# SwiGLU's token-tile features turned by VectorE and transfers, and three small moves between engines

## The chip, the core and the metric

The kernel runs on one core of one Trainium2 chip. The metric is the time of one execution on the device in microseconds (us); the median of three runs is given with their range. A profile is taken of one further execution; its times are counted from the start of its span. Engine names in it: PE is TensorE (PEld its weight loads), DVE is VectorE, ACT is ScalarE, POOL is GpSimd, SP is SyncE, which here only issues transfers. A "q" behind a name is the engine's queue of instructions.

## What is computed

Two layers work on 256 tokens of 1024 features, all in float32. Each layer has a token mixer (a gMLP in layer 0, an mLSTM with four heads in layer 1), then a dense SwiGLU of width 2816, then a gated embedding; behind the mixer and behind the SwiGLU stands a layer norm over a scaled residual:

```python
for i in range(DEPTH):
    y = gmlp_mixer(x, ...) if i % 2 == 0 else mlstm_mixer(x, ...)
    x = layer_norm(ALPHA * x + y, ln1_g[i], ln1_b[i])
    x = layer_norm(ALPHA * x + swiglu(x, ffn_w_gate[i], ffn_w_up[i], ffn_w_down[i]), ln2_g[i], ln2_b[i])
    gate = sigmoid(x @ ple_w_gate[i] + ple_b_gate[i])
    x = x + gate * (p[i] @ ple_w_proj[i])

def swiglu(x, w_gate, w_up, w_down):
    return (silu(x @ w_gate) * (x @ w_up)) @ w_down
```

In the mLSTM each head forms a masked 256 x 256 matrix P of queries against keys (scaled by exponentials of the gates), multiplies it with the values, divides by a sum, normalises, adds a skip path, and is gated with silu(z) before the output projection.

## The kernel before

**Precision.** Every float32 product is made of three matmuls in the fast 32-bit format: each operand is split into a high and a low half, and high x high, low x high and high x low are added in PSUM. `split` (L153) does it: ScalarE copies the value into the high half, VectorE subtracts to get the low half (`sub` names another engine for the subtraction, `fast=True` lets VectorE do the copy too).

**Weights.** `weight_plan` lists all weight tiles in the order of use. `ahead` (L170 on) issues their loads from SP into four `raw` buffers (L176, 512 KB each; the first three in halves of 256 KB), up to eight tiles ahead, and splits them into six `w` buffers or eight `b8` buffers, up to four tiles ahead. A load waits until its `raw` buffer has been split.

**Who sets the order.** The program is traced in Python, and a planner then gives each engine a fixed queue: among instructions that it holds ready by its own estimate it takes the one that comes first in the program, and it inserts the waits. `issue_after` and `manual_schedule` fix the order in a few places.

**The start.** After a few warm-up matmuls the input x, transposed on the host, comes in four pieces of two blocks (L359 on). ScalarE issues the load of block 0 (L363). `second_x` (L364) is called by `ahead` right after the first half of the first weight, so SP's queue begins: weight 0 first half, x block 1, weight 0 second half, x piece 1, weight 1 in two halves. L376 to L384 split these by hand: ScalarE copies x, VectorE or ScalarE copies the weight's half, VectorE subtracts. The matmuls at L422 use them.

**SwiGLU.** `channel_mixer` (L517). The first 512 of the 2816 features are made with tokens on the partitions: `first(t)` (L542) runs 48 matmuls for each token tile t of 128 tokens (gate, then up; the last eight of each at L289), and gives `hn[t]` = silu(gate) * up, 128 tokens x 512 features (L552, L553). The down projection needs features on the partitions. `transpose_h(t)` (L559) therefore transposes the four 128 x 128 blocks of `hn[t]` on TensorE into PSUM and splits each (128 x 128) into `hs[0..3]`. `transpose_h(0)` stands before the loop over f, `transpose_h(1)` after `gate_up(4)`. The other features, f = 4 to 21, are made by `gate_up(f)` with features on the partitions: eight matmuls each at L260 for `pg` and `pu`, then eight each at L264, then sums, silu, product and split. `Down` (L291 on) adds blocks into four PSUM banks at L240 to L242 (high, low, high of the activations); L240 and L242 load the high half of `h` as weights, L241 the low half. Blocks 0 to 3 are all added at f = 5, later blocks two steps behind `gate_up`.

**The mLSTM.** Under `manual_schedule` for ScalarE, L917 multiplies P of head h (128 x 384, causal blocks only) with its exponentials, and L920 splits it with the subtraction on GpSimd (`plo`). `pv_block(h)` (L930) multiplies with the values (L937 to L939; L939 takes `plo`), takes statistics on VectorE (L957 on), and lets ScalarE write the normalised `hn` (L967), which frees the PSUM banks `num`. `h_block(h)` (L971) transposes `hn` on TensorE (L976), adds the skip path on VectorE (L980), multiplies with silu(z) on VectorE (L981) and splits. `h_block(0)` runs behind `pv_block(2)`. After the last head, `Down` adds the 16 blocks; the first three wait for each other and are added together.

Of the kernel before, what the change touches and what calls it, by code (L numbers as in the profile page):

```python
# [12 lines left out]
ALU = mybir.AluOpType  # L13

P = 128
# [28 lines left out]
TOK = [slice(0, P), slice(P, 2 * P)]  # L44
# [11 lines left out]
def down_blocks(f):  # L56

    return range(4) if f == 3 + LAG else [f - LAG] if f > 3 + LAG else []
# [6 lines left out]
def stationary(key):  # L65

    return key[0] in ("u", "xm") and len(key) == 2 or key[0] in ("g", "u", "z") and key[-1] >= 4


def paired(key):  # L70

    return key[0] in ("g", "u") and len(key) == 3 and key[-1] >= 4 or key[0] == "u" and len(key) == 2
# [61 lines left out]
def trunk(ctx, tc, a, out):  # L134
    nc = tc.nc
    pe, act, dve, pool, sp = nc.tensor, nc.scalar, nc.vector, nc.gpsimd, nc.sync
# [8 lines left out]
    def tl(tag, shape, dt=F32, name="t"):  # L145
        return sb.tile(shape, dt, tag=tag, name=name, bufs=BUFS[tag])

    def bank(which, shape, name="ps"):
        return (psA if which == "A" else psB).tile(shape, F32, tag=which, name=name)

    def split(hi, lo, src, fast=False, sub=dve):

        return dve.tensor_copy(hi, src) if fast else act.copy(hi, src), sub.tensor_tensor(lo, src, hi.bitcast(F32), ALU.subtract)  # L153
# [14 lines left out]
    at = {"load": 0, "cast": 0, "use": 0}  # L168

    def ahead(loads, casts):  # L170
        while at["load"] < min(len(plan), at["use"] + loads):
            ap = plan[at["load"]][1]
            n = ap.shape[-1]
            t = tl("raw", [P, n], name="raw")
            for c in HALF if at["load"] < 3 else [slice(0, n)]:
                at["dma"] = sp.dma_start(t[:, c], ap[:, c])  # L176
                if at["load"] == 0 and c.start == 0:
                    second_x()
            raws[at["load"]] = t
            at["load"] += 1  # L180
        while at["cast"] < min(len(plan), at["use"] + casts):
            i = at["cast"]
            key, raw = plan[i][0], raws.pop(i)
            n = raw.shape[-1]
            if key in WIDE:
                t = tl("b8", [P, 2, D], F32R, "w")
            else:


                first = ASIDE if stationary(key) and not paired(key) else 0  # L190
                step = D + ASIDE if paired(key) else D
                t = tl("w", [P, 2 * D + P], F32R, "w")[:, first:first + 2 * step]
                t = t.rearrange("p (i n) -> p i n", i=2)[:, :, :D]
            with issue_after(behind["cast"]):
                if key[0] == "bdv":

                    t = t.rearrange("p i n -> p (i n)")[:, :4 * 2 * GW].rearrange("p (j i n) -> p j i n", j=4, i=2)
                    split(t[:, :, 0, :P], t[:, :, 1, :P], raw.rearrange("p (j n) -> p j n", j=4))
                    f = 4 * key[1]
                    pool.tensor_copy(t[:, :, :, P:], wx[:, f:f + 4, :].rearrange("p j (i n) -> p j i n", i=2))  # L200
                for c in () if key[0] == "bdv" else HALF if i < 3 else [slice(0, n)]:
                    split(t[:, 0, c], t[:, 1, c], raw[:, c])
            wt[i] = t
            at["cast"] += 1
# [18 lines left out]
    ident = sb.tile([P, P], F32, name="ident")  # L223
# [97 lines left out]
    def transpose_x(t):  # L321
# [5 lines left out]
            end = split(xh[:, 4 * j:4 * j + 4, TOK[t]], xl[:, 4 * j:4 * j + 4, TOK[t]], tp)  # L327
        return end

    def ln_residual(t, ps, g, b):  # L330
        x = xn[t]
        st = tl("c", [P, 2, 6], name="st")
        for j in range(2):
            c = HALF[j]
            dve.scalar_tensor_tensor(x[:, c], x[:, c], ALPHA, ps[j], ALU.mult, ALU.add)
            dve.bn_stats(st[:, j, :], x[:, c])
        mv = tl("c", [P, 2], name="mv")
        dve.bn_aggr(mv, st)
        rs = tl("c", [P, 1], name="rs")
        rsqrt(rs, mv[:, 1:2])  # L340
        for j in range(2):
            c = HALF[j]
            dve.scalar_tensor_tensor(x[:, c], x[:, c], mv[:, 0:1], g[:, c], ALU.subtract, ALU.mult)
            end = dve.scalar_tensor_tensor(x[:, c], x[:, c], rs, b[:, c], ALU.mult, ALU.add)
        behind["cast"] = (end,)

    def load_row(ap, n=D):
        t = tl("row", [P, n], name="row")
        sp.dma_start(t, ap.partition_broadcast(P))
        return t  # L350
# [7 lines left out]
    xr = []  # L358
    for i in range(4):  # L359
        t = tl("m2", [P, 2, S], name="xr")  # L360
        if i == 0:

            act.dma_start(t[:, 0, :], a["xT"][i, :, 0, :])  # L363
            second_x = lambda: sp.dma_start(xr[0][:, 1, :], a["xT"][0, :, 1, :])  # L364
            xr.append(t)
        else:
            sp.dma_start(t, a["xT"][i])
            xr.append(t)
        ahead(1 + i, 0)
    make_identity(nc, ident)  # L370
    pool.memset(mhalf, -0.5)
    with tc.manual_schedule(engines={mybir.EngineType.Activation, mybir.EngineType.DVE}):

        for i in range(2):
            w, raw = tl("w", [P, 2 * D + P], F32R, "w")[:, :2 * D].rearrange("p (i n) -> p i n", i=2), raws.pop(i)
            for k, h in enumerate(HALF):  # L376
                c = 2 * i + k
# [9 lines left out]
    for i in range(2, 4):  # L387
        c = slice(2 * i, 2 * i + 2)
# [4 lines left out]
    for c in range(6):  # L393
# [20 lines left out]
        for kp in range(4):  # L414
            w = weight("v", c, kp)
            for kk in range(2):
                k = 2 * kp + kk
# [11 lines left out]
        for t in range(2):  # L429
            o = vs[c][:, t, :]  # L430
# [22 lines left out]
    hs = {}  # L453
# [63 lines left out]
    def channel_mixer(l, acc, last, hook=None):  # L517
# [38 lines left out]
        hn = [first(0, lambda: transpose_x(1)), first(1)]  # L556
        hs = {e: tl("h", [P, 2, S], F32R, "h") for e in range(4)}

        def transpose_h(t):  # L559
            tp = bank("B", [P, 4, P], "tp")  # L560
            for e in range(4):
                pe.transpose(tp[:, e, :], hn[t][:, e * P:(e + 1) * P], ident)
            for e in range(4):
                split(hs[e][:, 0, TOK[t]], hs[e][:, 1, TOK[t]], tp[:, e, :])

        def gate_up(f):
            s, y = tl("s", [P, S], name="s"), tl("s", [P, S], name="y")
# [17 lines left out]
            hs[f] = tl("h", [P, 2, S], F32R, "h")  # L585
            split(hs[f][:, 0, :], hs[f][:, 1, :], s)

        transpose_h(0)
        rows = []
        for f in range(4, NF + LAG):  # L590
            if f < NF:
                gate_up(f)
            if f == 4:
                transpose_h(1)
                acc = Down(NF)
            for e in down_blocks(f):
                acc.add(e, hs.pop(e), weight("d", l, e, casts=1 if f >= NF else None))
            if f in (8, 10, 12):

                with issue_after([at["dma"]]):  # L600
                    rows.append(load_row(a[("ln2_g", "ln2_b", "ple_b")[f // 2 - 4]][l]))
            if f == 14 and hook:
                hook()
            if f == NF - 1:
                ahead(LOAD_AHEAD, LAG + 1)
# [96 lines left out]
    def mlstm(embed1):  # L702
# [32 lines left out]
        sz = [tl("b8", [P, 8, S], name="sz") for _ in range(2)]  # L735
# [97 lines left out]
        for s in range(NI + 3):  # L833
            if s < NI:
                y = xm_block(s)
# [23 lines left out]
        with tc.manual_schedule(engines={mybir.EngineType.Activation}):  # L859
# [43 lines left out]
            for h in range(NH):  # L903
                if h == 1:
                    z_copy(*z)
                    z = z_mm(11)
                gb = gbs[h // 2][:, h % 2]
                gm = tl("s", [P, 2, P], name="gm")
                dve.tensor_tensor(gm, gb, cmask.unsqueeze(1).to_broadcast([P, 2, P]), ALU.add)
                e = tl("m2", [P, 384], name="e")  # L910
                act.activation(e[:, 0:P], gm[:, 0, :], AF.Exp, bias=cols[:, 0, h:h + 1], scale=-1.0)
                act.activation(e[:, P:S], gb[:, 1, :], AF.Exp, bias=cols[:, 0, h:h + 1], scale=-1.0)
                act.activation(e[:, S:384], gm[:, 1, :], AF.Exp, bias=cols[:, 1, h:h + 1], scale=-1.0)
                if h == 1:
                    act.activation(cols[:, 2:4, :], cols[:, 2:4, :], AF.Exp, scale=-1.0)
                p = sc[h]
                dve.scalar_tensor_tensor(p, p, DH ** -0.5, e, ALU.mult, ALU.mult)  # L917
                hi = tl("h", [P, 384], F32R, "phi")
                lo = tl("h", [P, 384], F32R, "plo")
                split(hi, lo, p, sub=pool)  # L920
                ph.append((hi, lo))
            z_copy(*z)
            act.activation(sz[1][:, 0:4, :], sz[1][:, 0:4, :], AF.Silu)
# [1 line left out]
        hn = []  # L925
# [43 lines left out]
        hs = {}  # L969

        def h_block(h):  # L971
            for j in range(2):
                tp = bank("B", [P, 2, S], "tp")
                for i in range(2):
                    for t in range(2):
                        pe.transpose(tp[:, i, TOK[t]], hn[h][:, t, (2 * j + i) * P:(2 * j + i + 1) * P], ident)  # L976
                for i in range(2):
                    f = 4 * h + 2 * j + i
                    y = tl("s", [P, S], name="y")
                    dve.scalar_tensor_tensor(y, tp[:, i, :], par[:, f, 6:7], a1[f // 8][:, f % 8, :], ALU.mult, ALU.add)  # L980
                    dve.tensor_tensor(y, y, sz[f // 8][:, f % 8, :], ALU.mult)  # L981
                    hs[f] = tl("h", [P, 2, S], F32R, "h")
                    split(hs[f][:, 0, :], hs[f][:, 1, :], y)

# [119 lines left out]
```

## Time and profile before

| | |
|---|---|
| median of three runs | 825.69 us (825.42 to 826.16) |
| the profiled execution's own time | 825.63 us |
| its span | 823.9 us |
| granted TensorE clock, mean | 1.00 |
| bytes moved | 155.52 MB, 189 GB/s over the span |

The page gives, for each engine, the time in which it was busy, its share of the span and the number of its instructions. Matmuls are pipelined, so the busy times of single ones overlap: the distance between two starts says what one costs. The chain of waits follows back from the last instruction, at each step to what released it or to the instruction before it on its engine; its rows give start, length and what it was. In the timeline a row gives start, length, engine, line, operation, the tile written and the tiles read, and in brackets how long the engine had been idle before and what released it. A row of `SPq` is the issue of a transfer by SP; the time until the data has landed stands in the list of transfers.

### The profile page before, as it was taken

What the parts mean: (1) busy time and instruction counts of PE and PEld (TensorE: products, weight loads), DVE (VectorE), ACT (ScalarE), POOL (GpSimd) and SP (SyncE); (2) the same over time, 40 slices, a digit from 0 to 9 for tenths busy, and PEclk for the clock granted to TensorE, in tenths of its full rate; (3) what the DMA queues carried; (4) which work ended last, traced back from release to release, by engine and by line L of the source; (5) the groups of instructions that cost most, each with busy time, mean ns of one, the idle gap of its engine ahead of it and who ended that gap; (6) DMA issues with size and microseconds to landing.
All of it is one profiled execution on the core that took longest, in us unless ns stands there. A gap on an engine that the chain in (4) does not pass through costs nothing.

```text
span 823.9 us, 12407 instructions
## 1 busy us (share of the span) xinstructions
PE 816.9 (99%) x4520; PEld 708.0 (86%) x4520; DVE 614.3 (75%) x982; ACT 470.9 (57%) x820; POOL 149.6 (18%) x209
## 2 busy tenths in 40 slices
PE   9999999999999999999999999999999999999997
PEld 6888888888888888888889999988888888888886
DVE  6757998678956567586878998889885656776674
ACT  6656666565535556475256788776444555665522
POOL 1020643342000000700001677330000000000000
PEclk9999999999999999999999999999999999999999
DMA  8895447567176678677144355454626667886501
GB/s 287 283 337 182 153 159 225 179 194 243 67 260 202 192 225 281 201 229 252 38 146 156 135 162 161 146 177 147 215 90 224 196 199 228 269 264 212 179 1 51
DMA packets 44997, 155.52 MB, mean 189 GB/s; under 512 B 5256, under 2 KB 6024, under 8 KB 44936
## 3 DMA queue, kind: packets, MB, share of 16 engines
q1 hardware_dynamic: 44792, 154.60, 57.6%
q8 instruction: 35, 0.57, 0.3%
q14 instruction: 26, 0.21, 0.1%
q10 hardware_dynamic: 144, 0.13, 0.0%
HBM read 153.67 MB, written 1.05 MB: 188 GB/s over the span
## 4 chain that ended last, share of the span: by engine, by line
PE 96%; DVE 1%; ACT 1%; DMA 1%; issue 0%; POOL 0%; SPq 0%; DVEq 0%; ACTq 0%
PE acc L240 9%; PE acc L241 9%; PE acc L242 9%; PE pu L260 8%; PE pg L260 8%; PE ups L260 5%; PE pg L264 4%; PE pu L264 4%; PE ups L264 3%; PE vps L242 2%; PE vps L240 2%; PE vps L241 2%; PE xmps L245 2%; PE xmps L247 2%; PE xmps L246 2%; PE gate L289 2%
## 5 line engine op out<-in xcount | busy, mean ns | idle before, releaser
L153 DVE TENSOR_TENSOR w<-raw,w 128x1024 fp32r<-128x1024 f32 (+1 forms) x275 | 333.2, 1219 | 74.7 <-ACT w L153 73.1
L153 ACT CAST w<-raw 128x1024 fp32r<-128x1024 f32 (+1 forms) x275 | 284.9, 1046 | 120.6 <-PE acc L242 25.7
L240 PE MATMUL acc<-w,h 128*128 128x512 f32 x336 | 133.0, 396 | 0.2 <-ACT hn L967 0.2
L241 PE MATMUL acc<-w,h 128*128 128x512 f32 x336 | 131.3, 391 | 0.0
L242 PE MATMUL acc<-w,h 128*128 128x512 f32 x336 | 131.0, 390 | 0.0
L242 PEld LDWEIGHTS acc<-w,h 128*128 128x128 f32 x336 | 63.1, 188 | 13.9
L240 PEld LDWEIGHTS acc<-w,h 128*128 128x128 f32 x336 | 63.1, 188 | 12.1 <-ACT hn L967 0.6
L241 PEld LDWEIGHTS acc<-w,h 128*128 128x128 f32 x336 | 63.1, 188 | 11.2 <-DVE h L153 0.2
L260 PE MATMUL pg<-xs,w 128*128 128x512 f32 x288 | 71.6, 391 | 0.0
L260 PE MATMUL pu<-xs,w 128*128 128x512 f32 x288 | 71.5, 390 | 0.0
L260 PEld LDWEIGHTS pg<-xs,w 128*128 128x128 f32 x288 | 53.8, 188 | 11.0
L260 PEld LDWEIGHTS pu<-xs,w 128*128 128x128 f32 x288 | 53.8, 188 | 11.0
L319 POOL TENSOR_TENSOR rs<-ve,mhalf 128x1 f32<-128x1 f32 x8 | 7.6, 956 | 295.9 <-DVE ve L318 291.3
L271 ACT COPY s<-pg 128x256 f32<-128x256 f32 x36 | 13.4, 372 | 69.7 <-PE pg L264 69.7
L260 PE MATMUL ups<-xs,w 128*128 128x512 f32 x192 | 47.9, 391 | 0.0
L272 DVE TENSOR_TENSOR s<-s,pg 128x256 f32<-128x256 f32 x36 | 15.1, 421 | 42.8 <-ACT s L271 42.7
L260 PEld LDWEIGHTS ups<-xs,w 128*128 128x128 f32 x192 | 35.7, 188 | 7.2
L264 PEld LDWEIGHTS pg<-xs,w 128*128 128x128 f32 x288 | 38.9, 188 | 3.1
L264 PE MATMUL pg<-xs,w 128*128 128x256 f32 x288 | 39.5, 280 | 0.0
L264 PE MATMUL pu<-xs,w 128*128 128x256 f32 x288 | 39.4, 279 | 0.0
L264 PEld LDWEIGHTS pu<-xs,w 128*128 128x128 f32 x288 | 36.5, 188 | 0.3
L245 PE MATMUL xmps<-xs,w 128*128 128x256 f32 x128 | 36.3, 284 | 0.0
(252 smaller groups left out, 1635.7 us busy)
## 6 DMA issues: line engine op xcount, KB each, us to landing
raw<-in_ffn_g SPq DMA_DIRECT2D x44, 512.0 KB, 4.4
raw<-in_ffn_u SPq DMA_DIRECT2D x44, 512.0 KB, 4.6
raw<-in_ffn_d SPq DMA_DIRECT2D x44, 512.0 KB, 4.3
raw<-in_gm_u SPq DMA_DIRECT2D x24, 512.0 KB, 3.5
raw<-in_gm_wo SPq DMA_DIRECT2D x24, 512.0 KB, 3.4
raw<-in_gm_v SPq DMA_DIRECT2D x21, 512.0 KB, 5.2
raw<-in_ple_gate SPq DMA_DIRECT2D x16, 512.0 KB, 4.5
raw<-in_ml_z SPq DMA_DIRECT2D x16, 512.0 KB, 3.8
```

The costliest lines, as they stand in the source:

```text
L153: return dve.tensor_copy(hi, src) if fast else act.copy(hi, src), sub.tensor_tensor(lo, src, hi.bitcast(F32), ALU.subtract)
L240: pe.matmul(ps, lh, w[:, 0, c], start=start, stop=False)
L241: pe.matmul(ps, ll, w[:, 0, c], start=False, stop=False)
L242: pe.matmul(ps, lh, w[:, 1, c], start=False, stop=stop)
L245: pe.matmul(ps, w[:, 0, c], h, start=start, stop=False)
L246: pe.matmul(ps, w[:, 0, c], l, start=False, stop=False)
L247: pe.matmul(ps, w[:, 1, c], h, start=False, stop=stop)
L260: pe.matmul(ps, w[:, 0, k * P:(k + 1) * P], xs[:, k], start=k == 0, stop=False)
L264: pe.matmul(ps[:, 0], w[:, 1, k * P:(k + 1) * P], xh[:, k, :], start=False, stop=k == KD - 1)
L271: act.copy(o, ps[:, 1])
L272: dve.tensor_tensor(o, o, ps[:, 0], ALU.add)
L289: pe.matmul(ps, xl[:, k, TOK[t]], w[:, 0, c], start=False, stop=k == KD - 1)
```

## The change

Four edits:

1. **SwiGLU's token-tile features.** `transpose_h` goes, and its eight transposes on TensorE per layer with it. `square(y, t, hn[t])` is one VectorE instruction for each token tile: it transposes each 32 x 32 square of the 128 x 512 tile in place of its partition group, and orders the result by square column. `regroup` then moves the squares between partition groups with 16 transfers inside SBUF, issued by SP: each moves 32 partitions x 2 token tiles x 512 bytes, 32 KB. All 16 read what both squares wrote. The four splits (`split_h`, 128 x 256 each, from SBUF instead of PSUM) are placed after `gate_up(5)`, ahead of the blocks 0 to 3 of `Down`.
2. **P part of head 0.** The subtraction that gives the low half of P goes from GpSimd to VectorE for head 0.
3. **Gate of head 0.** The four multiplications with silu(z) go from VectorE to GpSimd for head 0.
4. **x's second block.** ScalarE issues its load, right behind that of the first; SP's queue loses it.

```diff
@@ ahead
             for c in HALF if at["load"] < 3 else [slice(0, n)]:
                 at["dma"] = sp.dma_start(t[:, c], ap[:, c])
-                if at["load"] == 0 and c.start == 0:
-                    second_x()
@@
+    def square(y, t, src):
+
+        dve.transpose(y[:, t].rearrange("p j k b -> p k j b"), src.rearrange("p (k j a) -> p k j a", k=4, j=4))
+
+    def regroup(o, y):
+
+
+        for j in range(4):
+            for i in range(4):
+                sp.dma_start(o[32 * j:32 * j + 32, :, i], y[32 * i:32 * i + 32, :, j])
@@ the start
         if i == 0:
-
-            act.dma_start(t[:, 0, :], a["xT"][i, :, 0, :])
-            second_x = lambda: sp.dma_start(xr[0][:, 1, :], a["xT"][0, :, 1, :])
+            for k in range(2):
+                act.dma_start(t[:, k, :], a["xT"][i, :, k, :])
@@ channel_mixer
-        def transpose_h(t):
-            tp = bank("B", [P, 4, P], "tp")
-            for e in range(4):
-                pe.transpose(tp[:, e, :], hn[t][:, e * P:(e + 1) * P], ident)
-            for e in range(4):
-                split(hs[e][:, 0, TOK[t]], hs[e][:, 1, TOK[t]], tp[:, e, :])
+
+        y = tl("row", [P, 2, 4, 4, 32], name="hsq")
+        for t in range(2):
+            square(y, t, hn[t])
+        ht = tl("row", [P, 2, 4, 4, 32], name="ht")
+        regroup(ht, y)
+
+        def split_h(e):
+            h = hs[e].rearrange("p i (t g b) -> p i t g b", t=2, g=4)
+            split(h[:, 0], h[:, 1], ht[:, :, :, e])
@@
-        transpose_h(0)
         rows = []
         for f in range(4, NF + LAG):
             if f < NF:
                 gate_up(f)
             if f == 4:
-                transpose_h(1)
                 acc = Down(NF)
+            if f == 5:
+                for e in range(4):
+                    split_h(e)
@@ mlstm
-                split(hi, lo, p, sub=pool)
+
+                split(hi, lo, p, sub=pool if h else dve)
@@ h_block
-                    dve.tensor_tensor(y, y, sz[f // 8][:, f % 8, :], ALU.mult)
+
+                    (dve if h else pool).tensor_tensor(y, y, sz[f // 8][:, f % 8, :], ALU.mult)
```

## The prediction

> **What bounds the kernel.** I read the page first (busy shares, chain by engine), then TensorE's waits, then the chain of waits, and the timeline around each edited place.
>
> ```profile
> span 823.9 us, 12407 instructions
> ...
> PE 816.9 (99%) x4520; PEld 708.0 (86%) x4520; DVE 614.3 (75%) x982; ACT 470.9 (57%) x820; POOL 149.6 (18%) x209
> ...
> PE 96%; DVE 1%; ACT 1%; DMA 1%; issue 0%; POOL 0%; SPq 0%; DVEq 0%; ACTq 0%
> ```
>
> TensorE works in 99% of the span and carries 96% of the chain. So only two things shorten the time: fewer TensorE instructions, and fewer of its waits. Those are few (engine, line <- releaser, total us, times, longest):
>
> ```profile
> PE vps L422 <- ACT w L382: 0.6, 1, 0.6
> PE num L939 <- POOL plo L153: 0.5, 1, 0.5
> ...
> PE acc L240 <- ACT hn L967: 0.2, 1, 0.2
> ```
>
> Each belongs to one of the small edits: the start, the P part of head 0, the gate. The big edit takes TensorE work away. The sum is made against the profiled execution, which took 825.63 us (span 823.9, and 1.73 around it); the median of the three runs shown, 825.69, is 0.06 from it. About 0.2%, 1.65 us, can be told from no change: below 824.04 is faster, above 827.34 slower.
>
> **Transposes taken from TensorE.** Each layer loses two groups of four transposes, ahead of `gate_up(4)` and ahead of the first `Down`. Busy time overstates them, since matmuls overlap; the chain shows what they hold up (start, us, what):
>
> ```profile
> 240.55 1.82 PE first L289 x8
> 242.81 1.85 PE pg L260 x8
> ...
> 247.43 0.94 PE pu L264 x8
> 248.80 1.84 PE pg L260 x8
> ...
> 265.24 1.81 PE pg L260 x8
> ...
> 630.84 1.82 PE first L289 x8
> 633.10 1.85 PE pg L260 x8
> ...
> 637.71 0.94 PE pu L264 x8
> 639.08 1.84 PE pg L260 x8
> ```
>
> From the end of one group to the start of the next: 242.81 - 242.37 = 0.44, 248.80 - 248.37 = 0.43, and in the second layer 0.44 and 0.43. The eight matmuls behind a transpose take 1.85 or 1.84 against 1.81 undisturbed (265.24), 0.03 or 0.04 each. Sum: 1.74 + 0.14 = **1.88 us less**, 0.94 in each layer. Nothing hides it: the engine goes straight on.
>
> **What replaces them.** Two passes of VectorE turn squares of 32, 16 transfers regroup the squares, and four splits (ScalarE copy, VectorE subtract) feed the first `Down` block at f = 5. All 16 need the second token tile's square, and block 0 needs all 16. Rows of the first layer:
>
> ```profile
> 242.48 0.69 DVE L553 TENSOR_TENSOR hn<-hn,first 128x512 f32<-128x512 f32 x1 [6.47 <-PE first L289]
> 243.08 1.22 DVE L153 TENSOR_TENSOR w<-raw,w 128x1024 fp32r<-128x1024 f32 x1
> ...
> 244.33 0.33 SPq L176 DMA_DIRECT2D raw<-in_ffn_g  x1
> ...
> 250.94 0.41 ACT L153 CAST h<-s 128x256 fp32r<-128x256 f32 x1
> ...
> 254.06 0.19 PEld L240 LDWEIGHTS acc<-w,h 128*128 128x128 f32 x1
> ...
> 254.18 0.19 PEld L241 LDWEIGHTS acc<-w,h 128*128 128x128 f32 x1
> ```
>
> Small loads issued back to back by SP, and times from issue to landing (last column) of a weight load, of the quickest load and of a store:
>
> ```profile
> 236.41 0.43 SPq L675 DMA_DIRECT2D wc<-in_ml_wc  x1
> 236.89 0.42 SPq L690 DMA_DIRECT2D wk<-in_ml_wk  x1
> ```
>
> ```profile
> raw<-in_ffn_g SPq DMA_DIRECT2D x44, 512.0 KB, 4.4
> ...
> raw<-in_ml_bdv SPq DMA_DIRECT2D x4, 256.0 KB, 2.7
> ...
> out<-xn SPq DMA_DIRECT2D x2, 128.0 KB, 1.7
> ```
>
> The last hn is ready at 242.48 + 0.69 = 243.17. No row shows a square; I give it the 0.69 of L553, the nearest pass over 128x512: 243.86. From 236.41 to 236.89 the queue needs 0.48 an issue, so the 16th goes out 15 x 0.48 = 7.2 later, near 251.1. No row shows a transfer within SBUF; 32 KB lies nearest to the 128 KB store, so 1.7: landed at 252.8. One copy (0.41, the cast at 250.94) and one subtract, taken the same: high half at 253.2, low half at 253.6. TensorE wants the low half (L241) at 254.18 - 0.94 = 253.24, so it waits **0.4 us**. The other blocks have 12 matmuls of cover each. In the second layer the two `pg` groups lie 5.98 apart as here (5.99), so the same 0.4; **0.8 in all**. Bounds: nothing, if the transfers land 0.4 sooner (less than nothing is excluded, the transposes are already booked); above, 1.22 for a square behind the queued weight subtract at 243.08, and 2.7 for landing like a weight load (4.4 - 1.7): 4.3 a layer.
>
> A rule of the Trainium skill speaks against this edit: "DMA: Bandwidth & Descriptors", section "Rules for kernel authors", wants small transfers joined into one, since under 64 KB mostly overhead is paid. Its "Anatomy of one DMA" puts the fixed part at about 2.0 us (for transfers issued by GpSimd), which would make the wait by my estimate 0.8 a layer, not 0.4, and the sum 0.8 us worse; no row here shows 32 KB within SBUF.
>
> Behind the 16 issues stand weight loads on SP. The one at 244.33 would go out near 251.6, land near 256.0 (4.4), and be cast and subtracted by about 258.4 (two passes at 1.22 at most); its matmuls start at 265.24 - 0.94 = 264.3. That cover of 5.9 makes the delay free. The splits themselves are no more work than the eight per layer that go.
>
> **P part of head 0.** Three timelines, VectorE with the gate's row below it, GpSimd, TensorE:
>
> ```profile
> 533.34 0.54 DVE L917 SCALAR_TENSOR_TENSOR sc<-sc,e 128x384 f32<-128x384 f32 x1
> ...
> 535.60 1.36 DVE L917 SCALAR_TENSOR_TENSOR sc<-sc,e 128x384 f32<-128x384 f32 x1
> ...
> 555.00 0.76 DVE L981 TENSOR_TENSOR y<-y,sz 128x256 f32<-128x256 f32 x2
> ```
>
> ```profile
> 534.50 2.04 POOL L153 TENSOR_TENSOR plo<-sc,phi 128x384 fp32r<-128x384 f32 x1 [11.40 <-ACT phi L153]
> ```
>
> ```profile
> 535.74 0.40 PE L938 MATMUL num<-vn,phi 128*128 128x512 f32 x1
> 536.60 0.50 PE L939 MATMUL num<-vn,plo 128*128 128x512 f32 x1 [0.47 <-POOL plo L153]
> 536.94 0.39 PE L937 MATMUL num<-vn,phi 128*128 128x512 f32 x1
> ```
>
> A matmul of this size takes a step of 0.23 (1.82 for eight, above), so L939 would start at 535.97 and L937 at 536.20; L937 starts at 536.94. So 0.74 is lost. On VectorE the subtract costs about 0.54 (L917, same size, alone): from 534.50 to 535.04, before 535.97. **0.74 less**; 0.4 if one weight pass of 1.22 stands ahead (535.72 + 0.54 = 536.26, a wait of 0.29, and its shadow); nothing gained is the end above.
>
> **Gate of head 0.** VectorE loses four multiplications, 0.76 for two, so 1.5 us, ahead of the last head's statistics, on which TensorE's wait of 0.2 for `hn` hangs. I take **0.2 less**; nothing is the end above. GpSimd's own price, by a pass of the same size, and the first `Down` matmul of this layer:
>
> ```profile
> L477 POOL TENSOR_TENSOR sv<-sv,cf 128x256 f32<-128x256 f32 x22 | 22.9, 1042 | 72.0 <-ACT sv L476 72.0
> ```
>
> ```profile
> 560.15 0.48 PE L240 MATMUL acc<-w,h 128*128 128x512 f32 x1
> ```
>
> Three such passes from 555.00 are over at 558.1, their splits (0.82) at 559.0, ahead of 560.15, and the fourth is used after these. But the L917 rows, 0.54 alone and 1.36 beside GpSimd's 2.04, show that the two slow each other. In the Trainium skill, "SBUF — State Buffer", section "Who interferes with whom", says that a VectorE operation with two SBUF inputs and a GpSimd operation reading SBUF exclude one another; by that rule, these rows agree. It is a rival below.
>
> **x's second block.** SP, the chain and VectorE at the start:
>
> ```profile
> 1.24 0.42 SPq L364 DMA_DIRECT2D xr<-in_xT  x1
> 1.71 0.42 SPq L176 DMA_DIRECT2D raw<-in_gm_v  x1
> ```
>
> ```profile
> 1.71 4.98 DMA raw<-in_gm_v
> ...
> 7.39 4.38 PE vps L422 x18
> ```
>
> ```profile
> 8.09 0.43 DVE L380 CAST w<-raw 128x512 fp32r<-128x512 f32 x1
> ```
>
> The half weight that ends the wait is issued 0.47 sooner. At most 0.47 comes of it. If the transfers behind land when they did, the 18 matmuls run into the next cast: six of 0.23 after 6.92 end at 8.30, the cast at 8.52, so 0.25 is kept. On the other side, a block of x that lands late puts its copy (0.41) ahead of the weight's. I take **0.2 less**.
>
> **Sum.** 825.63 - 1.88 - 0.74 - 0.2 - 0.2 + 0.8 = **823.4**.
>
> **Rivals.** (1) The regrouped squares come late, in part: landing at 2.7 like the quickest load, 1.0 later than taken, waits of 1.4 a layer, 2.8 in all: 825.4, no change. For it: the ring is shared with weight loads, and SP's pitch has no row for so scattered a pattern. Against: by 251 the queue has issued only these for 7 us.
> (2) Slower: the first `Down` block waits for transfers that stand behind weight loads. Square behind the subtract at 243.08 (1.22), landing 4.4: 4.3 a layer, 8.6 in all, 831.2. It decides once the low half is later than 255.6, 2.37 past 253.24 (total wait 4.73); that is a landing 3.7 or more after the last issue. For it: the planner orders VectorE and SP by its own estimate. Against: the squares come earlier in the program than that cast.
> (3) GpSimd's gate blocks VectorE for its whole passes: 4.2 lost against 1.5 saved, the wait at the last head's `hn` grows by 2.7 instead of going: 823.4 + 0.2 + 2.7 = 826.3.
> (4) The small edits do nothing, because the planner puts the subtract behind other work and the weight lands as before: 825.63 - 1.88 + 0.8 = 824.55.
>
> **Chances.** Forecast (wait up to 0.7 a layer, 822.3 to 824.0): 0.56. Rival 1: 0.20. Rival 2: 0.14. Rival 3: 0.04. Rival 4: 0.06. The forecast alone is faster; rivals 1, 3, 4 fall within 0.2%, so 0.56, 0.30, 0.14. The range starts at 822.3 (no wait, start at 0.47: 825.63 - 1.88 - 0.74 - 0.2 - 0.47 = 822.34) and goes over rivals 1, 3 and 4 to 827.2, with rival 2 left out. The forecast's own range is 822.3 to 824.0.
>
> **What would show it.** Right: no transposes between `first` and `pg`, the groups of 8 back to back; no wait of `num` for `plo`; SP with 16 issues about 0.48 apart beginning near 244; TensorE at L240/L241 of f = 5 waiting 0.4 or less for `h`. Wrong: a wait of several us there in both layers, `ht` as the releaser of ScalarE's split, weight loads among the 16 issues, or VectorE passes stretched beside the gate on GpSimd.

## The result and the profile after

The changed kernel takes 829.82 us in the median (828.42 to 830.07, five runs); the kernel before, beside it on the same chip, 825.69 (825.24 to 826.16). The ratio is 1.0048 with a 95% interval of 1.0037 to 1.0058: slower by 4.1 us. The profiled execution took 829.82 us with a span of 828.1, 4.2 more than before. The page after:

```profile
span 828.1 us, 12416 instructions
...
PE 817.8 (99%) x4504; PEld 707.6 (85%) x4504; DVE 617.3 (75%) x975; ACT 470.7 (57%) x812; POOL 153.2 (18%) x212
...
PE 61%; DVE 5%; SPq 2%; DMA 2%; issue 2%; ACT 1%; POOL 0%; DVEq 0%; ACTq 0%; POOLq 0%
```

TensorE has its 16 instructions less (x4504), and still its share of the chain fell from 96% to 61%. That share says which path is followed back, not how much time is lost (the row sums to 73%); the waits do. TensorE's waits after (engine, line <- releaser, total us, times, longest):

```profile
PE acc L238 <- ACT hn L981: 2.2, 1, 2.2
...
PE pg L258 <- ACT w L153: 1.0, 2, 0.5
PE acc L238 <- ACT h L153: 0.9, 1, 0.9
```

The wait of `num` for `plo` is gone, as forecast. Those for `hn` (0.2 before), for a weight's cast and for `h` took its place. Following the same matmul through both traces tells where the time went (after against before): the start -0.4; SwiGLU of layer 0 +1.1; P part of head 0 -0.7; from there to layer 1's first block +4.0; SwiGLU of layer 1 +0.2. Sum +4.2.

**SwiGLU, layer 0.** Timelines of VectorE, SP, ScalarE and TensorE (start, length, engine, line, operation; in brackets idle time and releaser):

```profile
242.70 1.23 DVE L153 TENSOR_TENSOR w<-raw,w 128x1024 fp32r<-128x1024 f32 x1
243.84 0.70 DVE L330 STREAM_TRANSPOSE hsq<-hn 128x512 f32<-128x512 f32 x1
...
243.95 0.33 SPq L176 DMA_DIRECT2D raw<-in_ffn_g  x1
244.57 11.18 SPq L337 DMA_DIRECT2D ht<-hsq  x16
...
257.03 1.33 ACT L153 CAST h<-ht 128x256 fp32r<-128x256 f32 x4 [1.04 <-DMA ht<-hsq]
...
253.56 2.12 PE L258 MATMUL pg<-xs,w 128*128 128x512 f32 x8 [0.55 <-ACT w L153]
255.52 1.09 PE L262 MATMUL pg<-xs,w 128*128 128x256 f32 x8
257.49 0.73 PE L238 MATMUL acc<-w,h 128*128 128x512 f32 x2 [0.88 <-ACT h L153]
```

The square takes the 0.70 that was guessed, but behind a weight's subtract; the 16 issues take 11.2 us, 0.70 each; the first copy of `h` starts at 257.03, and the first `Down` at 257.49. TensorE was free for it at 252.9. In the planned order f=6's gate block now stands ahead of the first `Down`; that block wasn't ready either (0.55 for its weight's cast). So of 4.6 us of lateness 2.8 are filled with work (eight matmuls at 0.23, eight at 0.12); with the slower steps behind each wait, 2.0 are lost in the stage, against 0.94 saved.

**The mLSTM's end.** The three rows of ScalarE before, and the three that answer to them after:

```profile
535.59 1.05 ACT L153 CAST w<-raw 128x1024 fp32r<-128x1024 f32 x1
537.00 0.51 ACT L153 CAST phi<-sc 128x384 fp32r<-128x384 f32 x1 [0.36 <-DVE sc L917]
...
538.27 1.03 ACT L153 CAST w<-raw 128x1024 fp32r<-128x1024 f32 x1
```

```profile
536.64 1.06 ACT L153 CAST w<-raw 128x1024 fp32r<-128x1024 f32 x1 [0.30 <-DMA raw<-in_ml_wo]
537.94 1.05 ACT L153 CAST w<-raw 128x1024 fp32r<-128x1024 f32 x1 [0.24 <-DMA raw<-in_ml_wo]
538.89 0.51 ACT L153 CAST phi<-sc 128x384 fp32r<-128x384 f32 x1
```

Two weight casts now stand ahead of head 1's `phi`, and each waits for its load. `phi` of heads 1, 2 and 3 is 1.9, 2.2 and 2.6 us late, `hn` of head 3 1.7. At the end of that row of heads, TensorE before, then after:

```profile
564.78 0.39 PE L242 MATMUL acc<-w,h 128*128 128x512 f32 x1
565.35 0.50 PE L240 MATMUL acc<-w,h 128*128 128x512 f32 x1 [0.18 <-ACT hn L967]
```

```profile
564.42 0.39 PE L240 MATMUL acc<-w,h 128*128 128x512 f32 x1
567.02 0.50 PE L238 MATMUL acc<-w,h 128*128 128x512 f32 x1 [2.21 <-ACT hn L981]
...
567.98 0.63 PE L238 MATMUL acc<-w,h 128*128 128x512 f32 x1
568.40 0.63 PE L239 MATMUL acc<-w,h 128*128 128x512 f32 x1
```

The same by stretches of 5 us, before and then after; the granted clock (PEclk) is the third column from the right:

```profile
565.00:570.00 5.00, 4.82 (x21) 3.81 (x21) 4.55 (x9) 3.85 (x7) 0.00 (x0) 1.00 0.33 104
```

```profile
565.00:570.00 5.00, 2.98 (x8) 2.41 (x9) 4.45 (x12) 3.37 (x7) 0.44 (x1) 0.76 0.00 0
570.00:575.00 5.00, 5.00 (x21) 4.02 (x21) 3.85 (x5) 3.54 (x5) 0.00 (x0) 0.90 0.68 190
```

18 matmuls of `Down`'s first token tile are done when the second tile needs the banks that `hn` of head 3 frees; in the kernel before the planned order had 21 matmuls there. Counted from the end of the last step, TensorE stands idle for 2.4 us (0.3 before). `hn` being 1.7 late, three matmuls fewer (0.7), and `Down` itself beginning only 0.3 later make up that difference. Behind that idle time eight matmuls go at a step of 0.43 in place of 0.23, over 3.4 us, which is 1.6 us more.

### The profile page after: what moved, and what is told of

Same layout as the page of the kernel before. It is cut to its first block, busy times and chain, and to the rows that moved or that the text cites. A ratio compares the mean times of both kernels' runs of the same rounds, so it can differ in the third digit from the quotient of the medians.

```text
span 828.1 us, 12416 instructions
## 1 busy us (share of the span) xinstructions
PE 817.8 (99%) x4504; PEld 707.6 (85%) x4504; DVE 617.3 (75%) x975; ACT 470.7 (57%) x812; POOL 153.2 (18%) x212
## 4 chain that ended last, share of the span: by engine, by line
PE 61%; DVE 5%; SPq 2%; DMA 2%; issue 2%; ACT 1%; POOL 0%; DVEq 0%; ACTq 0%; POOLq 0%
PE pu L258 7%; PE acc L238 7%; PE pg L258 7%; PE acc L239 7%; PE acc L240 6%; PE pu L262 4%; PE pg L262 3%; SPq L337 2%; PE xmps L243 2%; PE xmps L245 2%; PE xmps L244 2%; PE gate L287 2%; PE gate L284 2%; PE gate L285 2%; DVE w L153 1%
## 5 line engine op out<-in xcount | busy, mean ns | idle before, releaser
L485 POOL TENSOR_TENSOR sv<-sv,cf 128x256 f32<-128x256 f32 x22 | 23.3, 1061 | 71.3 <-ACT sv L484 71.3
```

Source lines behind the costliest of these rows:

```text
L485: pool.tensor_tensor(sv, sv, cf, ALU.add)
```

## The experiments

All times are medians beside the kernel before on the same chip; the difference to it is in brackets. The theories in the expectations: **A**, the gate on GpSimd made `hn` of head 3 late; **B**, the P part on VectorE did, by the order of ScalarE's casts; **V**, what is left of that wait is VectorE's queue; **R**, the turning loses more than its transposes gained, because TensorE waits for `h` (**W**), because SP's queue holds up weight loads (**Q**), or because the transfers share the DMA engines with them (**C**).

### One edit undone, or done alone

`gate_back`, on the changed kernel: 828.01 us (+2.72).

```diff
-                    (dve if h else pool).tensor_tensor(y, y, sz[f // 8][:, f % 8, :], ALU.mult)
+                    dve.tensor_tensor(y, y, sz[f // 8][:, f % 8, :], ALU.mult)
```

> The changed kernel with head 0's gate product back on VectorE, the other three edits kept. Theory A (the gate on GpSimd: its four passes of 1.00 us hold back head 0's low halves on VectorE, which stand ahead of head 3's statistics, so hn of head 3 ends late, TensorE idles 2.2 us before the second half of Down's sums and then runs slowly): the 3.95 us lost between 541.79 and the next layer's first block go away almost whole, 829.8 - 3.9 = 825.9 us, and the wait of acc for hn is under 0.5 us. Theory B (the P part on VectorE changed the written order, so that two casts of mLSTM output weights go ahead of head 1's phi, wait for their DMAs and make every later head 1.9 us late): the wait stays above 1.5 us and the time stays at 829.3 to 829.8 us. If both are needed, something between: 827 to 828.5 us.

`ppart_back`, on the changed kernel: 827.03 us (+1.74).

```diff
-                split(hi, lo, p, sub=pool if h else dve)
+                split(hi, lo, p, sub=pool)
```

> The changed kernel with head 0's low half of P back on GpSimd, the other three edits kept. Theory A (the gate's move alone makes head 3's hn late): the 0.7 us that the P part gained at num of head 0 is given back, and the rest stays, 830.5 us, with the wait of acc for hn still near 2 us. Theory B (the P part's new place in the written order sends two weight casts ahead of head 1's phi): phi of head 1 is again about 1.9 us earlier, the wait of acc for hn falls under 0.5 us, and the time is 829.8 + 0.7 - 3.9 = 826.6 us.

`pe_transposes`, on the changed kernel: 828.06 us (+2.77). The function `transpose_h` of the kernel before comes back with its calls.

```diff
-        for t in range(2):
-            square(y, t, hn[t])
-        regroup(ht, y)
+        transpose_h(0)
...
+                transpose_h(1)
...
-                for e in range(4):
-                    split_h(e)
```

> The changed kernel with TensorE's transposes of SwiGLU's token-tile features back, the other three edits kept. Theory R (by the two traces the regrouping costs a net 1.2 us in the first layer and 0.2 us in the second): 829.8 - 1.4 = 828.4 us, and the 3.95 us at the mLSTM's end stay. Rival S (the regrouping gains 1.08 us as forecast and the loss comes from elsewhere in the stage): 829.8 + 1.1 = 830.9 us. Rival M (the mLSTM's lateness comes from the changed order of weight loads behind the regrouping): 829.8 - 1.4 - 3.9 = 824.5 us.

`turn_alone`, on the kernel before: 826.89 us (+1.60, ratio 1.0018, 1.0010 to 1.0027). Its edit is the same diff the other way round.

> The kernel before with the turning by squares and transfers alone. Theory R: 825.7 + 1.4 = 827.1 us, the first Down waiting about 0.9 us for the copies of h behind f=6's gate block. Rival S (the forecast's term): 825.7 - 1.1 = 824.6 us. If the transfers also set back the loads of the mLSTM's weights: over 828 us.

TensorE's waits, first without the gate's move, then without the P part's:

```profile
PE acc L238 <- ACT hn L981: 2.1, 1, 2.1
```

```profile
PE acc L238 <- ACT hn L981: 0.6, 1, 0.6
PE num L953 <- POOL plo L153: 0.4, 1, 0.4
```

The wait stays without the gate's move (2.1) and without the turning (2.2); without the P part's it falls to 0.6. A falls, B stands, though `gate_back`'s time is 1.3 under the least that B expected. For the turning R stands: with TensorE's transposes back, the same matching of traces gives 0.0 in both SwiGLU stages, and in `turn_alone` +1.3 and +0.3. The profile of `gate_back` adds something: the same idle time, and no slow matmuls behind it.

```profile
567.14 0.50 PE L238 MATMUL acc<-w,h 128*128 128x512 f32 x1 [2.13 <-ACT hn L981]
567.48 0.39 PE L239 MATMUL acc<-w,h 128*128 128x512 f32 x1
567.71 0.40 PE L240 MATMUL acc<-w,h 128*128 128x512 f32 x1
```

So the slow pace comes in some executions and not in others. In the changed kernel four of five executions have a mean granted clock of 0.997 and take 829.75 to 830.07; the fifth has 0.999 and takes 828.42. In `gate_back` it is one of five (0.998, 830.13; the others 827.33 to 828.42): its median is lower mostly by the share of such executions, and five each can't tell whether the gate has a part in that share. The traces agree: without the 1.6 us of slow pace the changed kernel's would be 2.6 us over the kernel before; `gate_back`'s, without slow pace, is 2.8 over.

The other edits alone, on the kernel before:

`ppart_alone`, `ppart_back`'s diff the other way round: 827.97 us (+2.34, 1.0020 to 1.0043); executions with a clock of 1.000 take 826.98 to 827.49, those with 0.997 or 0.998 take 828.46 to 829.93.

> The kernel before with head 0's low half of P on VectorE alone. Theory B (with it two weight casts are written ahead of head 1's phi on ScalarE, every later head is 1.9 us late and Down's second tile waits 2.2 us for hn of head 3, as in the run without the gate's move, where acc waited 2.1 us): num of head 0 comes 0.7 us earlier, the wait costs 2.1 us more than in the kernel before, 825.3 - 0.7 + 2.1 = 826.7 us, and about 828.3 us in executions in which the granted clock then falls. Rival (the wait needs the turning or the gate's move as well): 825.3 - 0.7 = 824.6 us, with acc waiting for hn under 0.5 us.

`gate_alone`, `gate_back`'s diff the other way round: 825.98 us (+0.35, 0.9995 to 1.0012), its wait for `hn` 0.6.

> The kernel before with head 0's gate product on GpSimd alone. Theory A (GpSimd's four passes hold back the low halves that stand ahead of head 3's statistics): acc waits 1 us or more for hn of head 3, 826.3 us or above. Theory B (the gate is no part of the loss: in the changed kernel its return moved the wait only from 2.2 to 2.1 us): 825.3 us within 0.4, the wait for hn under 0.6 us.

`x_alone`: 825.61 us (-0.02, 0.9991 to 1.0009).

```diff
-            act.dma_start(t[:, 0, :], a["xT"][i, :, 0, :])
-            second_x = lambda: sp.dma_start(xr[0][:, 1, :], a["xT"][0, :, 1, :])
+            for k in range(2):
+                act.dma_start(t[:, k, :], a["xT"][i, :, k, :])
```

> The kernel before with x's second block sent by ScalarE's queue alone. If the 0.82 us by which the first weight-carrying matmuls start earlier in the changed kernel is kept to the end: 825.3 - 0.8 = 824.5 us. If 0.28 us of it goes back to the weight loads within the first stage, as between the two traces: 824.8 us. If the first stage is bound by its weight loads alone: 825.3 us.

The four alone sum to 1.60 + 2.34 + 0.35 - 0.02 = 4.3, the whole change costs 4.1. That doesn't show that the edits are independent: the share of executions with the slow pace moves a median by up to 1.5 us, and undone, one at a time, gate, P part and turning give back 1.4, 2.4 and 1.4, in sum 5.2. Of the edits done alone, the expected sizes held within 1 us for B and the turning, and for the gate B's expectation just held. x's block gains nothing: in the six profiles with the edit the first row-by-row matmul of the gMLP starts at 10.7 to 11.4, in the 14 without it at 10.7 to 11.9. The means are 0.4 apart, the ranges overlap, and nothing of it shows in the time. So the start's -0.4 above isn't shown to be this edit's.

### Is it the order of the casts, and is it the wait alone?

`ppart_held`: the P part alone, and the casts from head 2's z on held behind head 1's `phi`. 825.86 us (+0.23).

```diff
-                split(hi, lo, p, sub=pool)
+                end = split(hi, lo, p, sub=pool if h else dve)[:1]
+                if h == 1:
+                    phi1 = end
...
+            if h == 2:
+                behind["cast"] = phi1
```

> The kernel before with head 0's low half of P on VectorE, and the casts of the weights from head 2's z on written to come after head 1's phi. Theory B: phi of head 1 starts within 0.5 us of the kernel before, acc waits under 0.5 us for hn, and the 0.7 us of the P part is kept: 824.6 us. Rival (the lateness comes from VectorE, which has 0.54 us more to do ahead of the P of head 1): acc still waits about 2 us for hn and the time is 826.7 us. A mishap that would show: a z block waits for its weight's cast, at most 1.1 us for one cast, 825.7 us.

`phi` of head 1 starts at 535.90, 2.1 of the loss are gone, so the order of the casts is shown to be the cause; but the 0.7 us don't come out, since a wait of 1.2 for `hn` is left. So only a part of what B expected held: the heads are earlier, and the statistics of head 3, behind VectorE's other work, are not (561.41, in the kernel before 560.92).

`held_lowpool`, on `ppart_held`: 826.84 us (+1.17).

```diff
-                    split(hs[f][:, 0, :], hs[f][:, 1, :], y)
+                    split(hs[f][:, 0, :], hs[f][:, 1, :], y, sub=dve if h else pool)
```

> The kernel with the low half of P on VectorE and the casts held behind head 1's phi, and with the low halves of head 0's h (not its gate) on GpSimd: nothing on VectorE waits for them, and 1.7 us less of VectorE's work stands ahead of head 3's statistics. Theory V (the 1.2 us that acc still waited for hn there are VectorE's queue ahead of head 3's statistics): the wait falls under 0.3 us and the 0.7 us of the P part come out: 0.7 us under the kernel before. Rival: the first blocks of Down wait for GpSimd's four passes of 1.0 us (about 4 us after the gate products, near 560.5 where the first block stands at 559.2), up to 1.3 us, and nothing is gained.

A miss. Counted from head 0's first `num`, the statistics of head 3 start 0.6 us earlier than in `ppart_held`, and `Down`'s second tile 0.5 earlier (30.1 us against 30.5), as V wanted. But the planned order now has 18 matmuls ahead of that tile where `ppart_held` has 23, about 1.1 us less to cover the wait, so it grows to 1.8. The rival's reason fails too: no wait for GpSimd. Of eleven executions six, at a clock of 0.999 or 1.000, take 825.66 to 826.84, and five, at 0.997 or 0.998, take 827.78 to 828.07.

`after_begin4`, on the changed kernel: 826.15 us (+0.79).

```diff
-                if f < 3:
+                if f < 4:
...
-                    for t in range(2) if f == 2 else ():
+                    for t in range(2) if f == 3 else ():
```

> The changed kernel with four blocks of Down, in place of three, run on the first token tile before the second tile is begun: six more matmuls, 6 x 0.228 = 1.4 us, stand ahead of the first one that needs the banks of head 3. Theory B (the largest loss of the changed kernel is TensorE's wait for hn of head 3, 2.2 us, and the slow pace after it): the wait falls to about 0.8 us, the granted clock stays at 1.00 behind it, and the time falls by 1.4 us of wait and, against the executions with the slow pace, by up to 1.6 us more: 826.8 to 828.4 us. Rival (the second tile's matmuls are late for another reason, such as the cast of a weight): the time stays within 0.5 us of 829.8.

```profile
PE acc L238 <- ACT hn L981: 0.8, 1, 0.8
```

Six matmuls more ahead of the wait take it to 0.8, as expected, and the loss from +4.13 to +0.79, by 3.3 us, 0.3 more than the most that I expected; all eleven executions have a clock of 0.999 or 1.000. So the wait with its slow pace is most of the loss of this stage, not all: from head 1 to layer 1's first block the profiled execution (the longest of the eleven) still loses 1.3 us of the 4.0. The rest of its loss is the turning's, less the P part's gain.

`held_begin4` and `held_low_begin4`: the same diff on `ppart_held` and on `held_lowpool`. 825.43 us (+0.07) and 825.02 us (-0.34, ratio 0.9994, 0.9986 to 1.0003).

> The kernel with the low half of P on VectorE and the casts held behind head 1's phi (825.9 us, a wait of 1.2 us for hn), with four blocks of Down on the first tile before the second. Theory V (the P part's 0.7 us are given back in the wait for hn and nowhere else): 1.4 us of matmuls cover the wait, which falls under 0.3 us, and 0.6 to 1.0 us under the kernel before. Rival (other waits behind it take up what is gained, such as for the cast of f=3's weights): within 0.3 us of the kernel before.

> The kernel with the low half of P on VectorE, the casts held, and head 0's low halves of h on GpSimd (its wait for hn was 1.8 us, with Down begun 1.7 us earlier than in the kernel before), with four blocks of Down on the first tile before the second. Theory V: 1.4 us of the wait are covered, 0.4 us stay, no fall of the granted clock: 1.0 to 1.5 us under the kernel before, the best version so far. Rival: Down's fourth block waits for GpSimd's last low half (it ended at 560.8 and is wanted near 562.5) or a weight's cast, within 0.3 us of the kernel before.

Waits of 0.9 and 0.5 for `hn` are left, and both times miss what V expected. The second is the best version found, and its interval doesn't exclude the kernel before. In its trace the P part gains 0.7 us at `num` and 0.3 are given back by layer 1's first block: about half of the forecast 0.7 is recovered there, with three edits around it.

### Why the turning loses

`turn_unread`: the kernel before, transposes and all, with squares and transfers into a tile that nothing reads. 825.57 us (0.00).

```diff
+        y = tl("row", [P, 2, 4, 4, 32], name="hsq")
+        for t in range(2):
+            square(y, t, hn[t])
+        ht = tl("row", [P, 2, 4, 4, 32], name="ht")
+        regroup(ht, y)
         def transpose_h(t):
```

> The kernel before, with TensorE's transposes as they are, and the squares and the 16 transfers done beside them into a tile that nothing reads: the transfers' cost to the others alone. Theory Q: the weight loads behind the transfers are late, gate blocks wait about 0.5 us a layer, +1.0 us. Theory W: nobody waits, 0 to +0.3 us.

The transfers as such cost nobody anything, though the weight loads stand behind them as in the changed kernel. In this order Q and C fall and W stands: the loss comes from `h` being late. It does so in two ways, by TensorE's wait for `h`, and by f=6's gate block that the planned order then puts first: in `turn_alone` it waits 0.5 us a layer for its weight's cast, which stands behind f=5's copy in ScalarE's order and starts at once when that is done, with no wait for a load.

`later_alone` and `turn_later`: `Down` begun one step later, without and with the turning.

```diff
-    return range(4) if f == 3 + LAG else [f - LAG] if f > 3 + LAG else []
+    return range(5) if f == 4 + LAG else [f - LAG] if f > 4 + LAG else []
...
-            if f == 5:
+            if f == 6:
                 for e in range(4):
                     split_h(e)
```

The first pair of lines is in both, the second in `turn_later` alone. 825.58 us (+0.01) and 837.50 us (+11.93).

> The kernel before with SwiGLU's Down begun one step later and nothing else, as the measure for the turning with a later Down. All theories: within 0.4 us of the kernel before, as the same matmuls stand in another order; more than that would be a price of the later Down itself (its blocks' weights are loaded and cast one step later, five blocks of Down in a row).

> The kernel before with the turning alone, and SwiGLU's Down begun one step later (blocks 0 to 4 together after f=6, the copies of h behind f=6's gate block), so that 5 to 6 us more of TensorE work lie ahead of the first block that needs h. Theory W (the loss of the turning is the wait of acc for h, 1.1 us in the longest, and all of TensorE's order around it): the wait for h is gone and the 0.94 us a layer that the transposes took is kept, against the kernel before of the same call by -1.9 + 1.0 for the two waits of a gate block for its weights = 0.9 us faster. Theory Q (the loss is the weight loads set back by 11 us of issues on SP's queue): the waits move to weights of later blocks, in sum 2 us or more, and the time is 1 to 2 us over the kernel before, as with the turning alone (+1.6).

The largest miss. No wait for `h` is left, as W expected, and the same 16 transfers, harmless where they were, now cost 12 us. SP, ScalarE and TensorE:

```profile
244.50 11.17 SPq L339 DMA_DIRECT2D ht<-hsq  x16
255.78 1.00 SPq L176 DMA_DIRECT2D raw<-in_ffn_d  x2
...
259.31 1.04 ACT L153 CAST w<-raw 128x1024 fp32r<-128x1024 f32 x1 [3.46 <-DMA raw<-in_ffn_d]
...
263.68 3.78 PE L260 MATMUL pg<-xs,w 128*128 128x512 f32 x8 [5.21 <-ACT w L153]
```

With `Down`'s first five weights loaded ahead of f=7's, TensorE reaches f=7 before SP has come back from the transfers: 5.2 us idle, the next eight matmuls in 3.78 us where eight took 2.0, and the like in layer 1. Four executions have a clock of 0.991 to 0.995.

`turn_pool` and `turn_pool_later`, on `turn_alone` and `turn_later`: 826.43 us (+0.86, executions from 825.38 to 828.47) and 829.39 us (+3.72).

```diff
-                sp.dma_start(o[32 * j:32 * j + 32, :, i], y[32 * i:32 * i + 32, :, j])
+                pool.dma_start(o[32 * j:32 * j + 32, :, i], y[32 * i:32 * i + 32, :, j])
```

> The kernel before with the turning alone, its 16 transfers issued by GpSimd, which does nothing in these stages, in place of SP. Theory Q: the weight loads are no longer behind the transfers, no gate block waits for weights (1.0 us in two waits with SP), and the time is 0.6 to 1.0 us under the turning alone's (+1.6 over the kernel before), so +0.6 to +1.0. Theory W: what decides is when the last transfer lands; if GpSimd issues one in 0.6 us as SP does, no change, +1.6; if it takes 1 us for one, 16 of them end 5 us later, and the first Down waits up to 5 us more a layer, 10 us over the kernel before.

> The kernel before with the turning alone, its transfers issued by GpSimd, and Down begun one step later. With SP's issues this later Down cost 12 us, two waits of up to 5.2 us for the weights of f=7's gate block. Theory Q (those weights stood behind 11.2 us of transfers on SP's queue): with GpSimd's queue these waits go, the copies of h are ready before the later Down, and the 1.9 us of the transposes less 1 us of weight waits are gained: 0.5 to 1.5 us under the kernel before. Rival C (the loads are late because the DMA engines are shared): the waits stay above 2 us a layer, 4 us or more over the kernel before.

GpSimd issues one in 0.53 us, but they land 4.2 us after issue (1.9 from SP). A gain of 0.7 in the median over SP's issues, with a wide spread: not settled. The two waits for weights stay (1.0 in sum), against Q. With the later `Down` these waits fall from 9.1 to 4.0: SP's queue was more than half of that loss, not all. What is left isn't a late load, against C: the casts that TensorE waits for (at 259.51 in layer 0) start behind f=6's copies in ScalarE's order, with no wait for a transfer.

`turn_two`, on `turn_alone`: 827.16 us (+1.49).

```diff
-                sp.dma_start(o[32 * j:32 * j + 32, :, i], y[32 * i:32 * i + 32, :, j])
+                (pool if i % 2 else sp).dma_start(o[32 * j:32 * j + 32, :, i], y[32 * i:32 * i + 32, :, j])
```

> The kernel before with the turning alone, its 16 transfers issued half by SP and half by GpSimd. Theory W (what the first Down waits for is the last of 16 transfers issued one after the other, 11.3 us long on SP and 9.7 us on GpSimd): with two queues the last issue comes about 5 us earlier, near 249.5, h's copies end near 253.5, no wait of acc for h is left, and with one wait of 0.5 us a layer of a gate block for its weights the time is 0.4 to 0.9 us under the kernel before. Rival C (the transfers share the DMA engines with the weight loads, and two queues make both land later): a landing over 4 us, acc waits as before, +0.9 to +1.6 us as with one queue.

```profile
244.71 5.83 SPq L339 DMA_DIRECT2D ht<-hsq  x8
...
257.24 0.41 ACT L153 CAST h<-s 128x256 fp32r<-128x256 f32 x1 [1.63 <-DVE s L599]
257.78 0.40 ACT L153 CAST h<-ht 128x256 fp32r<-128x256 f32 x1
```

Both expectations miss. The issues end at 250.5 and land in 2.4 to 2.7 us, near 253, as W wanted; the copies of `h` start at 257.78 all the same. On ScalarE they are written behind f=5's copy of `h`, which waits for VectorE. So the landing is only the first of two locks on `h`, the written order the second. And of TensorE's waits in this kernel only 0.2 are for `h`, 1.0 are those of f=6's gate block for its weight's cast: the order planned around a late `h` costs more here than the wait itself. A kernel that opens both locks and leaves f=6 in its place was not tried.

## Why the prediction was wrong, step by step

- **Transposes, -1.88.** Right: they are gone and the groups follow one another directly (`first` starts at 240.01, `pg` at 241.82, eight steps of 0.23 later).
- **The wait of the first `Down`, +0.4 a layer. This step failed first**: 2.0 and 1.2 us. Its terms: the square, taken right behind `hn` (242.78 in this trace), came 1.1 later, at 243.84 (behind the subtract that I had kept as a bound); 15 issues at 0.48, 7.2 in all, took 10.6; landing at 1.7 was 1.8 to 1.9, right. I took the pitch from two loads of whole rows, the nearest rows, and gave it no upper bound: the term with the largest multiplier (15) was the one without a range. Rival 2's size, 4.3 us of lateness, was about right (4.6), but by issue time, not landing; and the planner's f=6 block filled more than half of it, which neither the forecast nor the rival had. For the rule of the Trainium skill that I weighed ("DMA: Bandwidth & Descriptors", "Rules for kernel authors"): the small transfers were the loss, as it warns, by 0.59 us and more of issue each rather than by the fixed part.
- **Weight loads behind the issues, free.** Right in the order of this kernel (`turn_unread`, 0.00), and by little: one step later they cost 12 us.
- **P part, -0.74.** Right at its place: `num` of head 0 gained 0.71. **The step that failed is what stood behind it: I booked a local gain as a gain of the whole.** The low half's new engine changed the written order of ScalarE, `phi` of heads 1 to 3 was 1.9 to 2.6 us late, and TensorE waited 2.2 us where it had 0.2. Alone the edit costs 2.3 us. I had asked of this edit only whether VectorE had room. Why the planner exchanges the cast and `phi` isn't shown; that it does so in every kernel profiled with the edit, but those with the casts held, is.
- **Gate, -0.2.** No gain: alone +0.35, within the uncertainty. In that trace, counted from head 1's `num`, `hn` of head 3 is 0.3 earlier, as forecast; but 18 matmuls stand ahead of it in place of 21 (0.7), and the wait grows to 0.6. Rival 3's mechanism was in part there: the four passes on GpSimd took 1.00 us each, and VectorE's four low halves beside them 2.50 us in place of about 1.5; its 2.7 us of wait were not (2.1 without the gate's move, 2.2 with it).
- **x's second block, -0.2.** Nothing that can be measured.
- **No rival** had the slow pace of TensorE behind an idle time. The Trainium skill has it ("TensorE: Matmul & The Clock Gate", "Why this matters for your kernels"): gaps over about 3 us bring the half clock back. Here 2.3 and 2.4 us were enough in two traces, and not in two others with 2.3 and 2.4. The window that the Trainium skill calls "free-running" (same page, Part 1) would make it a matter of where the gap falls; the runs agree with that, and don't prove it.

## What to carry to other kernels

When one operation moves to another engine, and a planner writes the queues, compare the written order of every engine before counting the gain: here a subtract of 0.54 us on VectorE moved a cast on ScalarE and, in the net, cost three times what it saved. Price many small transfers by their issue time on the queue times their number, and ask which loads stand behind them and when these are wanted. A wait of TensorE near 2 us can be dearer than its length: cover it with matmuls that are ready (here six, by changing two numbers, won 3.3 us back), and count after each edit how many still stand ahead of it.

## What the runs showed of the hardware

- 16 transfers of 32 KB within SBUF, each 32 partitions to 32 others in pieces of 512 bytes, issued back to back by SP: 0.59 us for the median issue and 0.64 to 0.70 from one to the next on the average, where two loads of whole rows had 0.43 and 0.48; 1.9 us to landing. Issued by GpSimd: 0.53 us, 4.2 us to landing.
- A VectorE transpose of all 32 x 32 squares of a 128 x 512 float32 tile takes 0.70 us, as long as a two-input pass over it.
- After 2.4 and 2.3 us without a matmul TensorE's step went from 0.23 to 0.43 us for 3.4 us in the traces of the changed kernel (granted clock 0.76 over 5 us) and of `ppart_alone` (0.74). In those of `gate_back` and `pe_transposes` it did not, behind 2.3 and 2.4 us. The 1.6 us that this costs agrees with the 1.5 us between the two groups of times of the changed kernel and of `held_lowpool`, whose one trace, behind 2.0 us, is of the quicker group.
